# Hyena transform on one Trainium2 core: the first butterfly level and the last of the inverse summed in PSUM, and the output gate multiplied by x2 at the projection

## The chip, the core and the metric

The kernel runs on one core of one Trainium2 chip. The metric is the device time of one execution in microseconds (us); of several executions the median is taken. A core has TensorE (PE) for matmuls, VectorE (DVE), ScalarE (ACT) and GpSimd (POOL) for elementwise work, and DMA queues that SyncE (SP), ACT and POOL feed. Each engine works through its own list of instructions in order.

## What is computed

Two layers of a hybrid mixer over 1024 latent and 256 context tokens: an adaLN-modulated norm, one input projection whose columns feed four groups (a Hyena long convolution, an RWKV-7 scan, windowed and dense attention), a SiLU gate on each group's output, one output projection. The change concerns the Hyena group:

```python
def two_sided_fftconv(u, h_fwd, h_bwd, bias):
    ...
    U = jnp.fft.rfft(u, n=2 * L, axis=1)
    K = jnp.fft.rfft(k, n=2 * L, axis=0)
    y = jnp.fft.irfft(U * K[None], n=2 * L, axis=1)[:, :L]
    return y + u * bias

    zc = short_conv(z.astype(jnp.float32), conv_w.astype(jnp.float32))
    v, x1, x2 = jnp.split(zc, 3, axis=-1)
    y = x1 * two_sided_fftconv(v, h[:, 0, 0], h[:, 0, 1], bias[0])
    return x2 * two_sided_fftconv(y, h[:, 1, 0], h[:, 1, 1], bias[1])
```

The result of `hyena_branch` is multiplied by silu of its gate columns.

## The kernel before

**The stages of a layer.** `Proj` projects 128 columns at a time: three times eight matmuls per group of tokens (two groups of 512, and one of 256 in layer 0, which also carries the context), since each operand is split into a high and a low part (`chan`, L246). `conv` writes a block of short-convolved Hyena columns to `hy_d` in DRAM (blocks 0 and 1 are v, 2 and 3 are x1, 4 and 5 are x2); `gate` writes a block of gates to `gt_d`. Some of these blocks run beside the first RWKV stage (`phase_a`), four gate blocks beside the Hyena stage: `k.spread` ties each of their matmul groups to a mark that `k.mark` sets behind a Hyena matmul. After the Hyena stage come attention and the second RWKV stage.

**The Hyena stage** (`hyena`). A transform of length 2048 over 1024 tokens is cut into R = 8 residues of 128 tokens. The stage has four *units*: two convolutions (`o_`) times two halves of 128 channels (`hf`). One unit is

- `forward`: for each residue two 128x128 f32 matmuls with the tables `F` (L1394), cosine and sine, into PSUM banks of two residues. `pair` copies a bank to SBUF on ACT (L1211) and lets DVE form its sum and difference with the bank four residues on (L1213, L1215). `eight` does the other two butterfly levels on DVE (L1238 to L1242, then `odd`, L1227 to L1232, and `even`, L1219 to L1222) into `W`.
- the product with the filter's transform `Kf` on DVE (L1404 to L1407).
- back: four DVE sums and differences (L1410 to L1413), then `eight` again, *flipped*, into `Z`.
- `inverse`: for each residue two matmuls with the tables `IV` (L1436, or L1438 where the operands are swapped) and a DVE product with x1 (L1441) or, at the end, with the gate (L1443).

For the second convolution `inverse` loads the gate and x2 from DRAM and multiplies them on DVE (L1424); the result goes to `mix_d`.

The pool `sp` gives every tag a fixed number of buffers: the tag `s4`, of which `S`, `D` and `G` come, has two; `s2` (`AB`, `AB1`, `TU`) has five; a tile waits until the readers of the one before it in its buffer are done. PSUM has four banks here. The order on each engine is fixed when the program is built, by a scheduler. The rows below call a matmul of two f32 operands two records, so that eight matmuls of 128x128 read as x16.

In the text a *turn* is the stretch from one unit's flipped `eight` (its first instruction, L1238) to the next unit's; T is its start. There are three turns in a layer, six in all, and their places are those of the first view below.

Of the kernel before, what the change touches and what calls it, by code (L numbers as in the profile page):

```python
# [83 lines left out]
def setup(k, cp, dp):  # L84
# [23 lines left out]
    k.hy_d = dp.tile([768, TOK], F32, name="hy_d")  # L108
# [107 lines left out]
class Proj:  # L216
# [33 lines left out]
    def conv(w, blk, wi, dst, row, ctx, tanh_rows=0, pace=None):  # L250
# [19 lines left out]
    def gate(w, blk, row, ctx, pace):  # L270
# [898 lines left out]
def hy_consts(c):  # L1169
    f = np.float32  # L1170
    for nm, n, R in (("", L, R8), ("c", C, 2)):
# [14 lines left out]
        c["fw" + nm], c["iv" + nm] = np.ascontiguousarray(fw).astype(f), np.ascontiguousarray(iv).astype(f)  # L1186
        t = np.linspace(0.0, 1.0, n, dtype=f)[:, None]
# [10 lines left out]
class Dft:  # L1198
# [35 lines left out]
    def eight(s, out, S, D, flip):  # L1234
# [122 lines left out]
def hyena(k, l, kd, sp, pp):  # L1357
# [11 lines left out]
    for hf in range(2):  # L1369
        zc = tile_([2, n], "zc", 1)  # L1370
        nc.sync.dma_start(out=zc, in_=zd[:, 0:2, hf, 0:n])
        zv = zc.rearrange("q s (p r) -> q s r p", r=R)
# [9 lines left out]
    IV = tile_([R, 2, p], "IV", 1, p)  # L1382
    nc.sync.dma_start(out=IV, in_=A["iv"])

    def forward(o_, hf):
        u = U[hf]
        Kf = tile_([R, 2, 128], "Kf", 1, p)
        nc.sync.dma_start(out=Kf, in_=kd[o_, hf])

        def tr(rs):  # L1390
# [12 lines left out]
        t = tile_([R, 2, 128], "Z", 2, p)  # L1403
# [4 lines left out]
        Z = tile_([R, 2, 128], "Z", 2, p)  # L1408
# [5 lines left out]
        ft.eight(Z, S, D, True)  # L1414
        return Z

    def inverse(o_, hf, Z):
        if o_ == 0:
            u2 = tile_([R, 128], "u", 2, p)
        else:  # L1420
            gx = tile_([2, n], "zc", 1)
            nc.sync.dma_start(out=gx[:, 0], in_=k.gt_d[hf * 128:hf * 128 + 128, 0:n])
            nc.sync.dma_start(out=gx[:, 1], in_=zd[:, 2, hf, 0:n])
            TT(gx[:, 0], gx[:, 0], gx[:, 1], op=ALU.mult)  # L1424
            gv = gx[:, 0].rearrange("q (t r) -> q r t", r=R)
        for r0 in range(0, R, 4):
# [232 lines left out]
```

## Time and profile before

| | |
|---|---|
| median of 3 runs | 2482.23 us (2477.79 to 2485.27) |
| the profiled execution's own time | 2476.97 us |
| its span | 2475.0 us |
| PE busy | 2199.5 us (89%) |
| DVE busy | 1628.2 us (66%) |
| ACT busy | 1042.8 us (42%) |
| granted TensorE clock, mean | 0.938 of full speed |

The profile gives each instruction's start, its length and what ended the idle time ahead of it. Busy shares are means over stages that differ much, so a stage is read from its own rows: the windows view gives the busy time of each engine in a stretch, the timeline the instructions themselves. The column PEclk is the granted clock: 1.00 is 2.4 GHz, 0.50 is 1.2 GHz.

### The profile page before, as it was taken

The numbers are of one execution on the slowest core, as the hardware profiler recorded it, in microseconds if no ns is written. First come the engines' busy times: TensorE is split into PE (matmuls) and PEld (weight loads), VectorE is DVE, ScalarE is ACT, GpSimd is POOL, SyncE is SP. The second block draws the span as 40 slices with busy tenths as digits, with TensorE's granted clock in tenths as the row PEclk, the third lists the DMA queues.
The fourth block names the chain that finished last, engine by engine and source line by source line (L and its number), as shares of the span: only waits on it lengthen the run. The fifth ranks groups of instructions, "written<-read, shape, count | busy, mean of one in ns | idle before, by whom it ended". The sixth has DMA issues, their size and how long they took to land.

```text
span 2475.0 us, 44767 instructions
## 1 busy us (share of the span) xinstructions
PE 2199.5 (89%) x17048; PEld 1831.8 (74%) x17048; DVE 1628.2 (66%) x3913; ACT 1042.8 (42%) x2503; POOL 275.4 (11%) x408
## 2 busy tenths in 40 slices
PE   6799899999967799999898998989997659999898
PEld 3696689788756577886686887978776558877676
DVE  6975446578778566558543787565777886666753
ACT  5422233543210377666644322335432017766651
POOL 1000122100000000003122001321000000001212
PEclk9899999799988799999998998999898779999999
DMA  8225753676512646533443222445674155663432
GB/s 273 88 83 173 254 162 96 167 198 196 193 71 88 213 140 187 163 123 87 142 144 115 83 92 97 127 116 159 173 208 174 52 153 166 194 196 92 132 116 102
DMA packets 303763, 358.05 MB, mean 145 GB/s; under 512 B 121288, under 2 KB 245495, under 8 KB 298173
## 3 DMA queue, kind: packets, MB, share of 16 engines
q1 hardware_dynamic: 276712, 261.61, 34.7%
q0 software_dynamic: 11232, 70.78, 8.5%
q10 hardware_dynamic: 15604, 22.80, 2.9%
q8 instruction: 135, 2.21, 0.4%
q14 instruction: 80, 0.65, 0.1%
HBM read 226.27 MB, written 128.84 MB: 143 GB/s over the span
## 4 chain that ended last, share of the span: by engine, by line
PE 64%; DVE 11%; DMA 11%; ACT 5%; issue 4%; SPq 2%; POOL 0%; ACTq 0%; DVEq 0%; POOLq 0%
PE acc L246 16%; PE acc L340 9%; PE ops L1119 8%; PE O L1021 4%; PE pt L1011 3%; DMA st_d<-ST 3%; PE pk L1333 2%; PE S L980 2%; PE pr L1394 1%; PE S L981 1%; ACT P L995 1%; PE p_g L576 1%; PE mps L130 1%; DVE tmp L642 1%; DVE X L643 1%
## 5 line engine op out<-in xcount | busy, mean ns | idle before, releaser
L246 PE MATMUL acc<-hhi,wh 128*128 128x512 f32 (+1 forms) x896 | 218.5, 380 | 8.1 <-ACT wh L232 5.4
L246 PE MATMUL acc<-hlo,wh 128*128 128x512 f32 (+1 forms) x896 | 217.6, 375 | 0.0
L246 PE MATMUL acc<-hhi,wl 128*128 128x512 f32 (+1 forms) x896 | 208.8, 369 | 5.4 <-DVE wl L233 5.4
L985 DVE TENSOR_REDUCE st<-S 128x1 f32<-128x512 f32 (+1 forms) x320 | 171.8, 559 | 58.6 <-PE S L981 40.1
L995 ACT ACTIVATE P<-S,st 128x512 f32<-128x512 f32 (+1 forms) x320 | 184.1, 585 | 31.2 <-DVE st L988 26.5
L246 PEld LDWEIGHTS acc<-hhi,wh 128*128 128x128 f32 x896 | 158.5, 197 | 41.2 <-ACT wh L232 7.2
L246 PEld LDWEIGHTS acc<-hhi,wl 128*128 128x128 f32 x896 | 155.7, 190 | 33.4 <-DVE wl L233 5.7
L246 PEld LDWEIGHTS acc<-hlo,wh 128*128 128x128 f32 x896 | 157.9, 193 | 27.7 <-issue 1.7
L951 ACT COPY PT<-pt 128x512 f32<-128x512 f32 (+2 forms) x283 | 134.6, 501 | 84.2 <-PE pt L1011 83.1
L1011 PE MATMUL pt<-ident,P 128*128 128x128 f32 x976 | 158.4, 284 | 9.9 <-ACT P L995 6.5
L980 PE MATMUL S<-kp,qs 128*128 128x256 f32 (+2 forms) x384 | 141.4, 377 | 20.8 <-ACT P L995 19.4
L1011 PEld LDWEIGHTS pt<-ident,P 128*128 128x128 f32 x976 | 112.7, 143 | 39.4 <-issue 13.2
L1021 PE MATMUL O<-PT,V 128*64 128x256 f32 x976 | 135.3, 389 | 2.2 <-ACT PT L951 1.1
L981 PE MATMUL S<-kp,qs 128*128 128x256 f32 (+2 forms) x384 | 119.7, 325 | 2.9 <-DMA kp<-qk_d 2.9
L232 ACT ACTIVATE wh<-wr 128x1024 fp32r<-128x1024 f32 x58 | 60.9, 1058 | 104.9 <-PE acc L246 94.5
L980 PEld LDWEIGHTS S<-kp,qs 128*128 128x128 f32 x384 | 74.5, 194 | 40.4 <-ACT P L995 27.4
L1021 PEld LDWEIGHTS O<-PT,V 128*64 128x64 f32 x976 | 71.5, 138 | 43.6 <-issue 6.5
L258 ACT COPY zp<-acc 128x512 f32<-128x512 f32 (+1 forms) x66 | 34.6, 529 | 153.8 <-PE acc L246 107.8
L340 PE MATMUL acc<-wl,hhi 128*128 128x256 f32 x608 | 90.4, 289 | 5.5 <-POOL wl L233 5.5
L340 PE MATMUL acc<-wh,hhi 128*128 128x256 f32 x608 | 91.0, 291 | 2.0 <-ACT wh L232 2.0
L345 ACT ACTIVATE qx<-acc 128x256 f32<-128x256 f32 x76 | 29.2, 384 | 141.4 <-PE acc L340 139.9
L340 PE MATMUL acc<-wh,hlo 128*128 128x256 f32 x608 | 87.5, 285 | 0.0
(381 smaller groups left out, 5053.6 us busy)
## 6 DMA issues: line engine op xcount, KB each, us to landing
IN<-in_d POOLq DMA_DIRECT2D x18, 2048.0 KB, 9.7
wr<-in_w_in POOLq DMA_DIRECT2D x58, 512.0 KB, 4.6
mw<-in_mod_w SPq DMA_DIRECT2D x48, 512.0 KB
in_d<-BK SPq DMA_DIRECT2D x20, 512.0 KB
in_d<-AL SPq DMA_DIRECT2D x20, 512.0 KB
kp<-qk_d SPq DMA_DIRECT2D x32, 320.0 KB
qk_d<-qo SPq DMA_DIRECT2D x72, 128.0 KB
in_d<-GG SPq DMA_DIRECT2D x18, 512.0 KB
```

What stands on the lines that cost most here:

```text
L232: w.k.nc.scalar.activation(h, r, AF.Copy)
L246: nc.tensor.matmul(ps[:, :n], a[:, kc * 128:(kc + 1) * 128], b[:, kc, t0:t0 + n], start=(i == 0 and kc == 0), stop=(i == 2 and kc == 7))
L340: nc.tensor.matmul(ps[:, :256], x_[:, kc, t * 128:(t + 1) * 128], w_[:, kc, :], start=(n == 0 and kc == 0), stop=(n == 2 and kc == 7))
L951: nc.any.tensor_copy(o, i)
L980: nc.tensor.matmul(ps[:, w0:w0 + w], qs[:, hd % 2, hd // 2], kp[kv][0][:, t0:t0 + w], start=True, stop=False)
L981: nc.tensor.matmul(ps[:, w0:w0 + w], qs[:, hd % 2, hd // 2], kp[kv][1][:, t0:t0 + w], start=False, stop=not masks)
L985: TR(ng[:, i:i + 1], ps[:, :w0], axis=AX.X, op=ALU.max, negate=True)
L995: nc.scalar.activation(P[:, :w], ps[:, :w], AF.Exp, bias=gm, accum_out=den[:, i:i + 1])
L1011: nc.tensor.transpose(pt[:, i, :], P[:, i * 128:(i + 1) * 128], k.ident)
L1021: nc.tensor.matmul(O[kv * 64:kv * 64 + 64, 0], V[:, t, kv * 64:kv * 64 + 64], PTs[kv][:, i], start=(i == 0), stop=(i == nt - 1))
L1119: nc.tensor.matmul(ps, a[:, kc, :], b[:, kc, s], start=(n == 0 and kc == 0), stop=(n == 2 and kc == 7))
L1333: nc.tensor.matmul(ps[:, a, j], F[:, r, j, :], pm[j ^ dual][:, r, :], start=True, stop=True)
```

## The change

Forward: the sum and the difference of residues r and r + 4 are now formed in PSUM. For each of the first four residues two matmuls add u[r] and u[r + 4] (or its negative `un`, which ACT writes) into the same place, and ACT copies the bank to `S` or `D`; `pair` is no longer used here. Inverse: the flipped `eight` ends after its second level and returns `AB`, `AB1` and `G`; the last sums and differences are made by four matmuls a residue in place of two, with a second table of negated values `NIV`. `Z` is gone, so the matmuls read `s2` and `s4` tiles. The blocks of x2 stay in SBUF: `conv` returns the tile and `gate` multiplies the gate by it (new L280), in the order x2 block, its gate, x2 block, its gate; `hy_d` loses two of its six blocks, and the product in `inverse` goes. `zc` becomes two buffers of one row each.

```diff
     def gate(w, blk, row, ctx, pace, z=None):
...
+        if z is not None:
+            for t0, n, o in ((0, L, 1), (L, C, 3))[:2 if ctx else 1]:
+                nc.vector.tensor_tensor(gt[:, t0:t0 + n], gt[:, t0:t0 + n], z[:, t0 + o:t0 + o + n], op=ALU.mult)
...
     def eight(s, out, S, D, flip):
...
-        s.odd(out, TU, D[:, 0:2])
+        if not flip:
+            s.odd(out, TU, D[:, 0:2])
         s.TT(AB, S[:, 0::2], S[:, 1::2], op=ALU.add)
         s.TT(AB1, S[:, 0::2], S[:, 1::2], op=ALU.subtract)
-        s.even(out, AB, AB1[:, 0], AB1[:, 1])
+        if not flip:
+            s.even(out, AB, AB1[:, 0], AB1[:, 1])
+            return
+        G = s.twiddled(TU, D[:, 0:2])
+        return (AB[:, 0], AB[:, 1]), (AB1[:, 0], AB1[:, 1]), (G[:, 0, 0], G[:, 0, 1]), (G[:, 1, 0], G[:, 1, 1])
...
+        un = tile_([R // 2, 128], "un", 1, p)
+        nc.scalar.activation(un, u[:, R // 2:], AF.Copy, scale=-1.0)
+
+        def tr(out, rs, far):
+
             ps = bank("pr").rearrange("p (r j e) -> p r j e", r=2, j=2)[:p]
             for a, r in enumerate(rs):
                 for j in range(2):
-                    nc.tensor.matmul(ps[:, a, j], F[:, r, j, :], u[:, r, :], start=True, stop=True)
+                    nc.tensor.matmul(ps[:, a, j], F[:, r, j, :], u[:, r, :], start=True, stop=False)
+                    nc.tensor.matmul(ps[:, a, j], F[:, r + R // 2, j, :], far[:, r, :], start=False, stop=True)
             k.mark(1.0)
-            return ps
+            nc.scalar.activation(out, ps, AF.Copy)
...
-        ft.pair(S[:, 2:4], D[:, 2:4], tr((1, 3)), tr((5, 7)))
-        ft.pair(S[:, 0:2], D[:, 0:2], tr((0, 2)), tr((4, 6)))
+        tr(D[:, 2:4], (1, 3), un)
+        tr(D[:, 0:2], (0, 2), un)
+        tr(S[:, 0:2], (0, 2), u[:, R // 2:])
+        tr(S[:, 2:4], (1, 3), u[:, R // 2:])
...
-            gx = tile_([2, n], "zc", 1)
-            nc.sync.dma_start(out=gx[:, 0], in_=k.gt_d[hf * 128:hf * 128 + 128, 0:n])
-            nc.sync.dma_start(out=gx[:, 1], in_=zd[:, 2, hf, 0:n])
-            TT(gx[:, 0], gx[:, 0], gx[:, 1], op=ALU.mult)
-            gv = gx[:, 0].rearrange("q (t r) -> q r t", r=R)
+            gx = tile_([n], "zc", 2)
+            nc.sync.dma_start(out=gx, in_=k.gt_d[hf * 128:hf * 128 + 128, 0:n])
+            gv = gx.rearrange("q (t r) -> q r t", r=R)
...
-                for j in range(2):
-                    iv, x = IV[:, r0 + a, j, :], Z[:, BACK[r0 + a], j, :]
...
+                jobs = [(IV[:, r, j, :], P[:, j]) for j in range(2)] + [(neg(i, j), Q[:, m]) for i, j, m in x]
+                for i, (iv, x) in enumerate(jobs):
                     if o_ == 0:
-                        nc.tensor.matmul(ps[:, a], iv, x, start=(j == 0), stop=(j == 1))
+                        nc.tensor.matmul(ps[:, a], iv, x, start=(i == 0), stop=(i == 3))
...
-                    first = [("h", i) for i in range(6)] + [(0, i) for i in range(2)]
+                    first = [("h", i) for i in range(4)] + [("h", 4), (0, 0), ("h", 5), (0, 1)]
```

**The order on PE, the first turn of layer 0**, before. `pi` are banks of the inverse, `pr` banks of the next unit's forward transform, `acc` projection groups of the gate blocks:

```order
L246 MATMUL acc<-hlo,wh 128x512 x8
L246 MATMUL acc<-hhi,wl 128x512 x8
L1436 MATMUL pi<-Z,IV 128x128 x4
L1394 MATMUL pr<-u,F 128x128 x8
L1436 MATMUL pi<-Z,IV 128x128 x12
L1394 MATMUL pr<-u,F 128x128 x8
L246 MATMUL acc<-hhi,wh 128x256 x8
```

After the change the same place begins so (`s_6620` and `s_6621` are `AB` and `AB1`):

```order
L246 MATMUL acc<-hhi,wl 128x512 x8
L1466 MATMUL pi<-s_6620,IV 128x128 x6
L1466 MATMUL pi<-s_6620,NIV 128x128 x2
L1417 MATMUL pr<-u,F 128x128
L1418 MATMUL pr<-un,F 128x128
L1417 MATMUL pr<-u,F 128x128
L1418 MATMUL pr<-un,F 128x128
L1466 MATMUL pi<-G,IV 128x128 x2
L1466 MATMUL pi<-G,NIV 128x128
L1466 MATMUL pi<-G,IV 128x128
L1466 MATMUL pi<-s_6621,IV 128x128 x2
L1466 MATMUL pi<-s_6621,NIV 128x128
```

and, behind the rest of the inverse (32 matmuls in all) and of the forward transform (32, of which four stand in the middle above), ends so:

```order
L1418 MATMUL pr<-u,F 128x128
L1417 MATMUL pr<-u,F 128x128
L1418 MATMUL pr<-u,F 128x128
L246 MATMUL acc<-hhi,wh 128x256 x8
L246 MATMUL acc<-hlo,wh 128x256 x8
L246 MATMUL acc<-hhi,wl 128x256 x8
```

Before, half of the next unit's 16 forward matmuls stood ahead of most of the inverse, and 32 in all stood between the projection groups. Now all but four of its 32 forward matmuls stand behind the last of the inverse, and 64 stand between the projection groups.

**The order on DVE, the same turn**, before, from the last two instructions of `odd`'s first step to the next unit's first level (`s_66..` are `S`, `D` and `s2` tiles):

```order
L1227 SCALAR_TENSOR_TENSOR G<-s_6603,s_6596 128x512
L1228 SCALAR_TENSOR_TENSOR G<-s_6603,s_6596 128x512
L1221 TENSOR_TENSOR Z<-s_6602 128x2x128
L1222 TENSOR_TENSOR Z<-s_6602 128x256
L1231 TENSOR_TENSOR Z<-G 128x2x2x128
L1232 TENSOR_TENSOR Z<-G 128x2x256
L1213 TENSOR_TENSOR s_6641<-s_6653,pr 128x512
L1215 TENSOR_TENSOR s_6642<-s_6653,pr 128x512
L1441 TENSOR_TENSOR u<-pi,x 128x512 x2
L1238 TENSOR_TENSOR s_6673<-s_6642 128x256
L1239 TENSOR_TENSOR s_6673<-s_6642 128x256
L1213 TENSOR_TENSOR s_6641<-s_6667,pr 128x512
```

and now, from the flipped `AB` on:

```order
L1256 TENSOR_TENSOR s_6620<-s_6614 128x512
L1257 TENSOR_TENSOR s_6621<-s_6614 128x512
L1236 SCALAR_TENSOR_TENSOR G<-s_6622,s_6615 128x512
L1237 SCALAR_TENSOR_TENSOR G<-s_6622,s_6615 128x512
L1471 TENSOR_TENSOR u<-pi,x 128x512 x2
L1252 TENSOR_TENSOR s_6716<-s_6673 128x256
L1253 TENSOR_TENSOR s_6716<-s_6673 128x256
L1256 TENSOR_TENSOR s_6714<-s_6672 128x512
L1257 TENSOR_TENSOR s_6715<-s_6672 128x512
L1229 TENSOR_TENSOR W<-s_6714 128x256
L1230 TENSOR_TENSOR W<-s_6714 128x256
L1236 SCALAR_TENSOR_TENSOR G<-s_6716,s_6673 128x512
```

The ten instructions that wrote `Z` and formed the first level are gone. Between `G` and the next unit's second level DVE now has only the two products with x1 (L1471), and `AB` (L1256) of the next unit stands directly ahead of everything but `TU` (L1252, L1253).

## Rows read from the trace of the kernel before

**Rows 1.** Windows view, the six turns: each engine's busy us (instructions), PEclk, DMA share, GB/s.
```profile
714.02:744.04 30.02, 23.05 (x136) 20.84 (x136) 27.20 (x44) 3.81 (x6) 0.00 (x0) 0.89 0.15 56
744.04:773.52 29.48, 26.23 (x160) 24.16 (x160) 26.15 (x43) 3.14 (x6) 0.00 (x0) 0.88 0.16 57
773.52:805.11 31.59, 20.94 (x112) 18.71 (x112) 28.35 (x48) 2.37 (x4) 0.00 (x0) 0.85 0.37 104
1930.48:1961.07 30.59, 21.16 (x112) 18.96 (x112) 26.78 (x43) 3.43 (x5) 0.00 (x0) 0.78 0.15 52
1961.07:1990.82 29.75, 26.68 (x136) 23.51 (x136) 25.75 (x42) 2.96 (x5) 0.00 (x0) 0.86 0.15 43
1990.82:2024.21 33.39, 14.37 (x88) 13.05 (x88) 28.40 (x51) 1.77 (x3) 0.00 (x0) 0.75 0.56 162
```

**Rows 2.** Timeline, DVE and one ACT row, second turn of layer 0: start, us, engine, line, [idle before].
```profile
744.04 0.42 DVE L1238 TENSOR_TENSOR s<-s 128x256 f32<-128x256 f32 x1
...
745.31 0.68 DVE L1242 TENSOR_TENSOR s<-s 128x512 f32<-128x512 f32 x1
...
747.18 0.69 DVE L1228 SCALAR_TENSOR_TENSOR G<-s,s 128x512 f32<-128x512 f32 x1
...
751.70 0.69 DVE L1213 TENSOR_TENSOR s<-s,pr 128x512 f32<-128x512 f32 x1 [1.96 <-PE pr L1394]
...
754.31 0.69 DVE L1441 TENSOR_TENSOR u<-pi,x 128x512 f32<-128x512 f32 x1 [0.65 <-PE pi L1436]
...
755.20 0.59 ACT L1211 COPY s<-pr 128x512 f32<-128x512 f32 x1 [4.29 <-PE pr L1394]
...
756.77 0.68 DVE L1215 TENSOR_TENSOR s<-s,pr 128x512 f32<-128x512 f32 x1
...
773.52 0.42 DVE L1238 TENSOR_TENSOR s<-s 128x256 f32<-128x256 f32 x1
```

**Rows 3.** Timeline, PE, the same turn.
```profile
746.48 2.05 PE L1436 MATMUL pi<-Z,IV 128*128 128x128 f32 x8 [7.01 <-DVE Z L1219]
...
748.32 3.27 PE L1394 MATMUL pr<-u,F 128*128 128x128 f32 x16
...
751.43 2.84 PE L1436 MATMUL pi<-Z,IV 128*128 128x128 f32 x24
...
754.11 1.95 PE L1394 MATMUL pr<-u,F 128*128 128x128 f32 x16
...
755.81 1.20 PE L246 MATMUL acc<-hhi,wh 128*128 128x256 f32 x8
```

**Rows 4.** Timeline, first unit of layer 0 (two rows) and of layer 1 (two rows).
```profile
686.48 1.06 PE L1394 MATMUL pr<-u,F 128*128 128x128 f32 x8
...
693.07 1.23 DVE L1424 TENSOR_TENSOR zc<-zc 128x1024 f32<-128x1024 f32 x1 [16.05 <-DMA zc<-hy_d]
...
1906.47 4.57 PE L1394 MATMUL pr<-u,F 128*128 128x128 f32 x32
...
1911.87 1.23 DVE L1424 TENSOR_TENSOR zc<-zc 128x1024 f32<-128x1024 f32 x1 [0.44 <-DMA zc<-hy_d]
```

**Rows 5.** Windows view, 4 us stretches of the same turn.
```profile
744.00:748.00 4.00, 1.52 (x7) 1.55 (x8) 4.00 (x10) 0.00 (x0) 0.00 (x0) 0.53 0.04 15
...
752.00:756.00 4.00, 4.00 (x38) 4.00 (x37) 3.02 (x6) 0.59 (x1) 0.00 (x0) 1.00 0.02 4
```

**Rows 6.** Timeline of layer 0's last unit and what follows; last row from the chain.
```profile
797.26 6.16 SPq L932 DMA_DIRECT2D kp<-qk_d  x8
...
811.11 5.23 PE L1438 MATMUL pi<-IV,Z 128*128 128x128 f32 x24 [1.27 <-DVE Z L1232]
...
816.38 1.07 DVE L1443 TENSOR_TENSOR zc<-pi,zc 128x512 f32<-128x512 f32 x1 [1.20 <-PE pi L1438]
...
817.49 0.36 PE L980 MATMUL S<-kp,qs 128*128 128x256 f32 x1 [1.15 <-DMA qs<-qk_d]
...
821.06 19.32 DMA zc<-hy_d
```

More of the change, by code (lines that the diff above doesn't have):

```diff
@@ L268, in conv, with gate @@
             nc.sync.dma_start(out=dst[row:row + 128, 1024:TOK], in_=o[:, 1027:1283])
-    def gate(w, blk, row, ctx, pace):
+    def gate(w, blk, row, ctx, pace, z=None):
         k, nc, sp = w.k, w.k.nc, w.sp
@@ L284, in beside @@
     def beside(w, todo, part=None):
+        z = None
         ctx = not w.last
@@ L1186, in hy_consts @@
         c["fw" + nm], c["iv" + nm] = np.ascontiguousarray(fw).astype(f), np.ascontiguousarray(iv).astype(f)
+        if not nm:
+            at = [BACK.index(x) for x in range(R)]
+            c["niv"] = np.stack([-c["iv"][:, at[x], 1 - x % 2] for x in range(2, R)] + [-c["iv"][:, at[1], j] for j in range(2)], 1)
         t = np.linspace(0.0, 1.0, n, dtype=f)[:, None]
@@ L1222, in even, with twiddled @@
         s.TT(o[:, 5:7], A1[:, ::-1], B1, op=ALU.subtract)
-    def odd(s, out, TU, CD):
-        o = out.rearrange("p s j e -> p (s j) e")
+    def twiddled(s, TU, CD):
         G = s.sp.tile([128, 2, 2, 2, 128], F32, tag="s4", bufs=2, name="G")
@@ L1228, in odd @@
         s.STT(G[:, 1], TU, -RT, CD, op0=ALU.mult, op1=ALU.add)
+        return G
+    def odd(s, out, TU, CD):
+        o = out.rearrange("p s j e -> p (s j) e")
+        G = s.twiddled(TU, CD)
         g, h = G[:, :, 0], G[:, :, 1]
@@ L1369, in hyena @@
     for hf in range(2):
[L1370 to L1372 removed]
         for s, lst in ((0, U), (1, X1)):
+            zc = tile_([n], "zc", 2)
+            nc.sync.dma_start(out=zc, in_=zd[:, s, hf, 0:n])
+            zv = zc.rearrange("q (p r) -> q r p", r=R)
             u = tile_([R, 128], "ux"[s], 2, p)
@@ L1381, in hyena @@
         yield
-    IV = tile_([R, 2, p], "IV", 1, p)
+    IV, NIV = tile_([R, 2, p], "IV", 1, p), tile_([R, p], "NIV", 1, p)
     nc.sync.dma_start(out=IV, in_=A["iv"])
+    nc.sync.dma_start(out=NIV, in_=A["niv"])
     def forward(o_, hf):
@@ L1413, in forward @@
         TT(S[:, 2:4], W[:, 4:6], W[:, 6:8], op=ALU.add)
-        ft.eight(Z, S, D, True)
-        return Z
+        return ft.eight(None, S, D, True)
     def inverse(o_, hf, Z):
@@ L1432, in inverse @@
             for a in range(4):
-                for j in range(2):
-                    iv, x = IV[:, r0 + a, j, :], Z[:, BACK[r0 + a], j, :]
+                r, place = r0 + a, BACK[r0 + a]
+                g, h = place // 2, place % 2
+                neg = lambda i, j: NIV[:, place - 2 if g else 6 + j] if i else IV[:, r, j, :]
+                if g == 0:
+                    (P, Q), x = (Z[0][0], Z[0][1]), [(h, 0, 0), (h, 1, 1)]
+                else:
+                    P, Q = Z[g]
+                    x = [(h, 0, 1), (1 - h, 1, 0)]
+                jobs = [(IV[:, r, j, :], P[:, j]) for j in range(2)] + [(neg(i, j), Q[:, m]) for i, j, m in x]
+                for i, (iv, x) in enumerate(jobs):
                     if o_ == 0:
-                        nc.tensor.matmul(ps[:, a], iv, x, start=(j == 0), stop=(j == 1))
+                        nc.tensor.matmul(ps[:, a], iv, x, start=(i == 0), stop=(i == 3))
                     else:
-                        nc.tensor.matmul(ps[:, a], x, iv, start=(j == 0), stop=(j == 1))
+                        nc.tensor.matmul(ps[:, a], x, iv, start=(i == 0), stop=(i == 3))
             k.mark(2.0)
@@ L1446, in inverse @@
         else:
-            nc.sync.dma_start(out=k.mix_d[hf * 128:hf * 128 + 128, 0:n], in_=gx[:, 0])
+            nc.sync.dma_start(out=k.mix_d[hf * 128:hf * 128 + 128, 0:n], in_=gx)
     for o_ in range(2):
@@ L1512, in ctx_hyena @@
     zd = k.hy_d.rearrange("(s h p) t -> p s h t", h=2, p=128)
-    zc = tile_("zc", [3, 2, C])
-    for s in range(3):
+    zc = tile_("zc", [2, 2, C])
+    for s in range(2):
         nc.sync.dma_start(out=zc[:, s], in_=zd[:, s, :, L:TOK])
     gx = load(tile_("gx", [2, C]), k.gt_d[0:256, L:TOK].rearrange("(h p) t -> p h t", p=128))
-    TT(gx, gx, zc[:, 2], op=ALU.mult)
     ux = []
```

14 lines of the change are left out of this document (7 added, 7 removed).

## The prediction, made before the changed kernel was run

> **What bounds the kernel now.** I read the windows view of the Hyena stages first, then DVE's timeline of one turn, then PE's timeline beside it. On the average PE looks like the bound (89% of the span), but the Hyena stages are another matter: in the six turns DVE is busy for 25.8 to 28.4 of 29.5 to 33.4 us, PE for 14.4 to 26.7 [rows 1]. So a turn is DVE's, and that is what the change goes at. But PE is not far behind: 26.2 of 29.5 us in the second turn, at a granted clock of 0.88.
>
> The timeline shows where DVE does stop [rows 2]. T is 744.04. DVE works without a gap through the flipped `eight`, stops 1.96 us at 751.70 for the next unit's forward matmuls and 0.65 us at 754.31 for the inverse, and has finished the next unit's first level at 756.77 + 0.60 = 757.37, that is T + 13.3. From there to the next T, 773.52, it has work for 16.15 us, three or four gate products among it. PE starts the inverse at 746.48 and is through with inverse and forward at 756.06 [rows 3]: 32 matmuls in some 9.6 us, nearly all of it covered by DVE's own work on `Z`, the first level and the products with x1. **That cover is what the change removes together with the work.**
>
> What a matmul costs depends on the clock. The 24 records at 751.43 take 2.84 us, 0.237 us for each of 12 matmuls; the 24 ahead of them, 746.48 to 751.43, need 4.95 us, because PE had stood idle 7 us and comes back at the lower level: PEclk is 0.53 in the first 4 us and 1.00 from 752 [rows 3, 5]. At the lower level all along, 12 matmuls take 5.23 us, 0.436 us each [rows 6].
>
> **The change, part by part.**
>
> *What DVE loses.* A unit loses the four instructions of `pair`, the two of `odd`'s second step and the four of `even` in the flipped `eight`: 6 of 512 columns, which follow each other every 0.60 us, and 4 of 256, every 0.34: 5.0 us a unit, 40 us over eight units. That is the gain if nothing takes their place.
>
> *What PE gains.* 16 forward and 16 inverse matmuls more in a unit, 256 in all: at 0.237 us 61 us of PE. They are not free even beside DVE: the second turn's 26.2 us of PE would come to about 32 with 7.6 us more and the lower clock taken out, against a turn of 29.5.
>
> *A turn after the change.* The order says what must follow what. DVE makes `TU` and `AB`: in the trace the third instruction after T starts at 745.31, so `AB` stands at T + 1.27 [rows 2]. PE starts at about T + 1.4 with eight inverse matmuls that need only `AB`, then four forward ones, 24 inverse ones (`G` stands at T + 3.2, in time) and 28 forward ones: 64 with nothing between. At 0.237 us they end at T + 16.6. ACT copies the last bank: 0.59 us as in 755.20 [rows 2], with some 0.3 us for the two hand-overs (an estimate from the gaps of 0.1 to 0.2 us between these rows). `AB` of the next unit reads all of `S`, and the rest of DVE's list stands behind it, so DVE goes on at T + 17.5. `TU` and the products with x1 are done by then. The instructions from there to the next T are those of before, 16.15 us. So the first level stands at T + 17.5 in place of T + 13.3: **+4.2 us a turn, +25.2 us for six**, if PE has its full clock. Of DVE's 5.0 us nothing is left, since it waits.
>
> *The clock.* PE will come back from idle at the lower level in four of the six turns: in the third turn of each layer 96 or 72 projection matmuls follow the forward transform and last until 2 us before the next inverse; in the others it stands idle for 5 us or more by the same reckoning, and I take it to come back as it did after the 7.01 us at 746.48. The lower level cost 4.95 - 2.84 = 2.1 us there [rows 3]; it then was partly hidden, now it all lies on the path: 4 x 2.1 = +8.4. Its ends are 0 and 6 x 2.1 = 12.6.
>
> *The product with x2.* L1424 takes 1.23 us of DVE in the third turn of each layer: -2.4. In the first units it costs more: in layer 0 DVE stood at 693.07 for the load of x2, although the first sum's bank was ready before; in layer 1 it waited 0.44 us [rows 4].
>
> *The first units.* Layer 0: forward starts at 686.48 [rows 4] and T was 714.02 [rows 1], 27.5 us. Now 32 matmuls of 0.237, 0.9 for the copy and 16.15: 24.7, and 0.3 for a short lower clock: -2.5. Layer 1: 1906.47 to 1930.48 was 24.0 us; now the same, 24.6, and 0.9 for four matmuls at the lower level: +1.5. Together -1.
>
> *The tail.* The last unit's inverse runs alone. In layer 0 it ended 11.2 us after T (811.11 + 5.23 against 805.11) at the lower level [rows 1, 6]. Now 32 matmuls from T + 1.4: 15.4 us at the lower level all along, 12.2 if the second half runs at 0.237. I take +2 a layer, +4; the ends are 0 and 8.
>
> *At the projection.* L280 adds 1.23 us of DVE twice a layer (and 0.4 for the context in layer 0), beside projection matmuls that keep PE busy. I cost it at nothing; without that cover it is at most 6. Where `z` is held, the two `zo` buffers alternate as before.
>
> *Queues.* On SP the loads of v and x1 are four of 0.5 MB and `NIV` is one more of 0.5 MB a layer, ahead of `Kf` and the second half's loads; the two gate loads stand ahead of the later `Kf` loads and wait for transposes only. All that is issued while PE still works on projections: nothing, at most 2 us. Behind the stage, the context's Hyena part loads two blocks, not three, out of a wait of 19.32 us [rows 6]: -1, at most -3.
>
> Is a longer stage paid in full? In layer 0 the attention's first matmul waits for loads of `qs` that follow the loads of `kp`, and those were issued at 797.26, when the last projection group was done [rows 6]. That group is tied to the Hyena matmuls by its marks and so moves with them: yes.
>
> **The sum:** 25.2 + 8.4 - 2.4 - 1 + 4 - 1 = +33 us. The profiled execution took 2476.97 us, so 2510; it lies 5.3 us under the median of the runs, 2482.2, so I forecast **2515 us** for the median.
>
> **The rivals.**
>
> *The clock stays up.* Twice the matmuls might keep PE busy enough that it no longer falls to the lower level between units. Then the 8.4 us and half of the tail go: +23, 2505 us. For it: the full clock from 752 on, once PE is busy [rows 5]. Against it: the projections are no more than before and the turn gets longer, so there still are idle stretches like the 7.01 us at 746.48 [rows 3]. The Trainium skill has this rule in "TensorE: Matmul & The Clock Gate", section "What's actually happening": the throttled state is the default and activity releases it. The rows agree that it rises with work and falls with idleness; the rule would speak for this rival, with its +23.
>
> *The delay is swallowed behind layer 0.* There the chain waits 19.32 us for loads [rows 6]. If these came no later than now, layer 0's share, half of the sum, would vanish: +17, 2499 us. Against it: the loads are issued behind the last projection.
>
> *Gain and loss cancel.* A turn breaks even where 64 matmuls take 11 us, 0.172 us each. Neither row has such a price, but if the scheduler's order let DVE work ahead by a few us it would come to the same: within 7 us of 2482.
>
> *Faster: a matmul that adds into PSUM costs half.* If the second of two that go to the same place cost about one record, 0.118 us, the second half of the 64 would be 3.8 us shorter; if all did, 7.6 us: DVE's wait would end at T + 9.9, -3.4 a turn, -20 in six, with the other terms -25: 2457 us. It decides below 0.172 us. Against it: the inverse of before already adds two matmuls into each place, and its 0.237 us is the price of just that [rows 3].
>
> **How the numbers follow.** The forecast, PE's chain with the clock falling in most turns: 0.52. Clock up: 0.20. Swallowed: 0.13. Cancelled: 0.08. Faster: 0.07. About 0.3%, 7 us, is what a measurement of this kernel can tell from no change. So faster 0.07, same 0.08, slower 0.85. The range reaches down to the swallowed case and half of the way to no change, 2491, and up to 2532, where the lower clock and the tail take their upper bounds (+4, +4) and DVE waits 1.5 us more a turn for projection groups that now end later.
>
> **What would show it.** The turns grow to about 36 us, with DVE busy about 22 of them and one wait of some 12 us at the next unit's `AB` (L1256) or `TU` (L1252), put down to ACT L1420 or PE L1418. L1213 and L1215 with `pr` and L1424 are gone; PE has 512 more records of 128x128. The forecast is wrong if the DVE wait ahead of the second level is under 8 us, if the 64 matmuls of a turn take less than 13 us, or if the stage grows and the span doesn't.

## The result, and the profile after

The kernel became slower: 2527.9 us median (2516.9 to 2536.6), beside 2483.8 us (2477.8 to 2485.8) for the kernel before, both in four runs. The ratio is **1.0152, with a 95% interval of 1.0114 to 1.0190**, which is +38 us (28 to 47); the two medians themselves lie 44 us apart. The profiled execution of after has a span of 2515.1 us against 2475.0 us, 40.1 us more; it was the fastest of its four runs.

The first line of the page shows what was exchanged, work of DVE for work of PE:

```profile
PE 2253.6 (90%) x17560; PEld 1884.6 (75%) x17560; DVE 1591.4 (63%) x3837; ACT 1057.1 (42%) x2524; POOL 276.6 (11%) x408
```

PE has 17,560 matmul records where it had 17,048, which is the 512 of 256 more matmuls, and 54 us more of busy time. DVE has 37 us less. PE's share rose from 89% to 90%, and the time rose too.

The windows view of the six turns, after (span, then busy us and instructions of PE, PEld, DVE, ACT, POOL, then PEclk, DMA share, GB/s). It answers to [rows 1]:

```profile
721.33:758.49 37.16, 31.13 (x200) 28.92 (x200) 22.38 (x34) 5.55 (x9) 0.00 (x0) 0.87 0.12 47
758.49:793.33 34.84, 32.53 (x224) 30.46 (x224) 21.32 (x32) 4.87 (x9) 0.00 (x0) 0.94 0.13 49
793.33:826.38 33.05, 25.47 (x176) 23.23 (x176) 22.37 (x37) 3.59 (x6) 1.84 (x2) 0.97 0.20 54
1960.63:1996.73 36.10, 28.13 (x176) 25.91 (x176) 21.95 (x33) 5.17 (x8) 0.00 (x0) 0.88 0.13 45
1996.73:2030.64 33.91, 32.41 (x200) 29.46 (x200) 20.81 (x31) 4.10 (x7) 0.00 (x0) 0.92 0.13 45
2030.64:2063.49 32.85, 20.21 (x153) 18.72 (x152) 22.24 (x39) 3.58 (x6) 1.84 (x2) 0.89 0.35 96
sum 207.91, PE 169.88 PEld 156.70 DVE 131.08 ACT 26.86 POOL 3.69; mean PE 28.31 PEld 26.12 DVE 21.85 ACT 4.48 POOL 0.61
```

DVE is busy for 21 to 22 us of a turn, where it was busy for 26 to 28, and the turn is longer, not shorter: 207.9 us for six, against 184.8 in [rows 1], so +23.1. DVE was the engine that filled a turn; now neither is full.

Where DVE stands still, in its timeline of the first of these turns (start, duration, engine, line, tile; in brackets the idle time ahead of it and what ended it). It answers to [rows 2], one turn earlier:

```profile
721.33 0.42 DVE L1252 TENSOR_TENSOR s<-s 128x256 f32<-128x256 f32 x1
...
723.93 0.69 DVE L1237 SCALAR_TENSOR_TENSOR G<-s,s 128x512 f32<-128x512 f32 x1
731.24 0.69 DVE L1471 TENSOR_TENSOR u<-pi,x 128x512 f32<-128x512 f32 x1 [6.62 <-PE pi L1466]
733.92 0.69 DVE L1471 TENSOR_TENSOR u<-pi,x 128x512 f32<-128x512 f32 x1 [1.99 <-PE pi L1466]
735.49 0.43 DVE L1252 TENSOR_TENSOR s<-s 128x256 f32<-128x256 f32 x1 [0.88 <-ACT s L1420]
...
740.80 0.69 DVE L1256 TENSOR_TENSOR s<-s 128x512 f32<-128x512 f32 x1 [4.55 <-ACT s L1420]
741.41 0.69 DVE L1257 TENSOR_TENSOR s<-s 128x512 f32<-128x512 f32 x1
```

Four waits, 6.62 + 1.99 + 0.88 + 4.55 = 14.0 us, stand between T and the next unit's `AB`; those that [rows 2] shows come to 2.6 us. The first two, 8.6 us, stand ahead of the products with x1, which wait for the inverse; the last ends at `AB`. And what PE did meanwhile:

```profile
722.79 2.90 PE L1466 MATMUL pi<-s,IV 128*128 128x128 f32 x12 [7.97 <-issue]
725.49 1.06 PE L1466 MATMUL pi<-s,NIV 128*128 128x128 f32 x4
...
739.30 0.39 PE L1418 MATMUL pr<-u,F 128*128 128x128 f32 x2
739.52 0.39 PE L1417 MATMUL pr<-u,F 128*128 128x128 f32 x2
739.75 0.39 PE L1418 MATMUL pr<-u,F 128*128 128x128 f32 x2
739.89 1.20 PE L246 MATMUL acc<-hhi,wh 128*128 128x256 f32 x8
```

One chain of 64 matmuls runs without a stop from 722.79 to 739.89, and DVE's next `AB` (L1256, 740.80) comes 0.9 us behind its end. The duration of a record overlaps the next; the starts are 0.22 us apart, for the first product into a place (L1417) and for the one added to it (L1418) alike.

Over all eight units, the groups of DVE instructions (name, shapes, count, busy us, mean ns) with the idle time ahead of them in us, and what ended it:

```profile
L1256 DVE TENSOR_TENSOR s<-s 128x512 f32<-128x512 f32 x16 | 11.1, 691 | 36.5 <-ACT s L1420 36.5
L1252 DVE TENSOR_TENSOR s<-s 128x256 f32<-128x256 f32 x16 | 6.8, 424 | 30.8 <-ACT s L1420 30.8
L1471 DVE TENSOR_TENSOR u<-pi,x 128x512 f32<-128x512 f32 x8 | 5.5, 692 | 31.8 <-PE pi L1466 31.8
```

The three kinds of wait come to 99 us. Before, in the kernel's own lines, two kinds stood in their place:

```profile
L1213 DVE TENSOR_TENSOR s<-s,pr 128x512 f32<-128x512 f32 x16 | 11.0, 686 | 21.5 <-PE pr L1394 21.3
L1441 DVE TENSOR_TENSOR u<-pi,x 128x512 f32<-128x512 f32 x8 | 5.5, 692 | 3.0 <-PE pi L1436 3.0
```

That is 24.5 us, and 17 us more stood ahead of the product with x2, nearly all in the first unit of layer 0 [rows 4]. The change took 37 us of work off DVE and gave it some 58 us of waiting.

Of the 40.1 us between the two spans, 23.1 lie in the six turns. The rest, from the starts of the same lines in both traces: 3.7 up to the last `p_w` matmul of layer 0, 3.6 from there to the first T, 1.8 from the last T to the attention, 7.0 from the last `p_w` of layer 1 to the last copy of the solve, 4.6 from there to T, 0.5 behind the last T, 0.3 to the end; attention and all between the layers came out 4.6 shorter. No edit touches the code of the 3.7. In the 7.0 and the -4.6 there are edits, of the gate part: the products of L280 in layer 1 start at 1847.02 and 1883.42, and the context's Hyena part has one load and one product less. But the 7.0 is a stretch of 106.3 us before and 113.3 after, and over the profiled executions of this study, before and after among them, it takes 100.2 to 113.3 us, both ends of that in kernels with the gate part (e6 and the changed one). I take these three for variation, which is not shown for each of them; the other terms come to some 34 us.

### The profile page after: what moved, and what is told of

Its sections match the earlier page's. It is cut to its first block, busy times and chain, and to the rows that moved or that the text cites. A ratio compares the mean times of both kernels' runs of the same rounds, so it can differ in the third digit from the quotient of the medians.

```text
span 2515.1 us, 45718 instructions
## 1 busy us (share of the span) xinstructions
PE 2253.6 (90%) x17560; PEld 1884.6 (75%) x17560; DVE 1591.4 (63%) x3837; ACT 1057.1 (42%) x2524; POOL 276.6 (11%) x408
## 4 chain that ended last, share of the span: by engine, by line
PE 68%; DMA 11%; DVE 9%; ACT 5%; issue 4%; SPq 1%; POOL 0%; ACTq 0%; DVEq 0%; POOLq 0%
PE acc L246 18%; PE acc L347 9%; PE ops L1126 8%; PE O L1028 4%; PE pt L1018 3%; DMA st_d<-ST 2%; PE p_g L583 2%; PE S L987 2%; PE pk L1352 2%; ACT P L1002 2%; PE pi L1466 1%; PE S L988 1%; DMA zc<-hy_d 1%; PE pr L1417 1%; PE pr L1418 1%
## 5 line engine op out<-in xcount | busy, mean ns | idle before, releaser
L1002 ACT ACTIVATE P<-S,st 128x512 f32<-128x512 f32 (+1 forms) x320 | 184.2, 585 | 29.5 <-DVE st L995 24.8
L1018 PEld LDWEIGHTS pt<-ident,P 128*128 128x128 f32 x976 | 113.3, 143 | 37.9 <-issue 13.2
L352 ACT ACTIVATE qx<-acc 128x256 f32<-128x256 f32 x76 | 29.2, 385 | 144.6 <-PE acc L347 144.6
```

The costliest lines, as they stand in the source:

```text
L1002: nc.scalar.activation(P[:, :w], ps[:, :w], AF.Exp, bias=gm, accum_out=den[:, i:i + 1])
L1018: nc.tensor.transpose(pt[:, i, :], P[:, i * 128:(i + 1) * 128], k.ident)
```

## The experiments

The theory (**A**): the matmuls are added at a place where DVE has nothing to do but wait for them, so the loss is their chain's length. The main rival (**B**): the change has other DMA issues in another order, SP's loads come late, and the loss is ahead of the stage. Further rivals: it is the added PE work as such, or the clock.

**e1: the gate part alone** (before, with the edits of that part; these are the main ones):

```diff
-    k.hy_d = dp.tile([768, TOK], F32, name="hy_d")
+    k.hy_d = dp.tile([512, TOK], F32, name="hy_d")
...
+                nc.vector.tensor_tensor(gt[:, t0:t0 + n], gt[:, t0:t0 + n], z[:, t0 + o:t0 + o + n], op=ALU.mult)
...
-            nc.sync.dma_start(out=gx[:, 1], in_=zd[:, 2, hf, 0:n])
-            TT(gx[:, 0], gx[:, 0], gx[:, 1], op=ALU.mult)
```

> The kernel before with the gate part alone: hy_d of 512 rows, the product of gate and x2 at the projection, the order of the projections and one load less in inverse; the transform stays on DVE. Theory A (the transform's PE chain makes the loss): the turns keep their 30 us, the third turn of each layer loses the 1.2 us of the product: 2478 to 2484 us. Theory B (the other number and order of DMA issues makes the loss, through SP's waits ahead of the stage): the stage begins some 9 to 12 us later over the two layers: 2493 us or more.

Measured: 2485.4 us, ratio 0.9993 (0.9970 to 1.0016).

**e2: the transform alone**, the same edits undone in the changed kernel, and v and x1 of a half again in one load.

> The changed kernel with the gate part undone: hy_d of 768 rows, x2 loaded and multiplied in inverse, v and x1 in one load, the projections' old order; both transform levels in PSUM. Theory A: six turns of +4 us and the x2 product back on DVE, where it now falls into DVE's wait: 2507 to 2520 us. Theory B: 2484 to 2492 us.

Measured: 2520.2 us, ratio 1.0131 (1.0094 to 1.0169); its six turns take 213.6 us. The two together: the gate part is worth nothing that can be measured, and the whole loss is the transform's. The fewer stores and the missing loads of x2, a part of B's reason, are in e1 as well and do nothing there; the separate loads of v and x1 are not, and e4 goes at those.

**e3: half of the forward sum left out**, in the changed kernel:

```diff
-                    nc.tensor.matmul(ps[:, a, j], F[:, r, j, :], u[:, r, :], start=True, stop=False)
-                    nc.tensor.matmul(ps[:, a, j], F[:, r + R // 2, j, :], far[:, r, :], start=False, stop=True)
+                    nc.tensor.matmul(ps[:, a, j], F[:, r, j, :], u[:, r, :], start=True, stop=True)
```

> The changed kernel without the second matmul of each forward place (it leaves out half of the forward sum): 16 matmuls less in a unit, all else as it was. Theory A (DVE waits for PE's chain): at 0.223 us a matmul 3.6 us less in each of six turns and two first units, 28 us: about 2499 us, turns of 30 to 33 us. If DVE's own work or the queues set the turn: no change, 2520 to 2530 us.

Measured: 2495.4 us, ratio 1.0039 (1.0017 to 1.0060), that is 28 us under the changed kernel's 1.0152. Its turns in layer 0, in the windows view:

```profile
718.04:750.27 32.23, 26.21 (x168) 24.00 (x168) 22.37 (x33) 5.56 (x9) 0.00 (x0) 0.92 0.14 52
750.27:782.54 32.27, 29.95 (x192) 27.89 (x192) 21.33 (x33) 4.87 (x9) 0.00 (x0) 0.90 0.14 52
782.54:813.44 30.90, 23.33 (x144) 21.11 (x144) 22.37 (x36) 3.58 (x6) 1.91 (x2) 0.91 0.21 59
```

DVE's work is the same to 0.01 us as in the changed kernel, and PE has 16 matmuls less in a turn (32 records), so this version leaves out a part of the transform. The turns of layer 0 are 9.7 us shorter in sum, where 16 matmuls less at 0.223 us would make 10.7. So it is PE's chain that DVE's time hangs on, not its own work.

**e4: one load for v and x1**, in the changed kernel:

```diff
-            zc = tile_([n], "zc", 2)
-            nc.sync.dma_start(out=zc, in_=zd[:, s, hf, 0:n])
+        zc = tile_([2, n], "zc", 1)
+        nc.sync.dma_start(out=zc, in_=zd[:, 0:2, hf, 0:n])
```

> The changed kernel with v and x1 of a half loaded by one DMA into one tile, as before, which takes two issues off SP and gives the later loads another place in the rotation. Theory B: the second half's transposes no longer wait 10 and 22 us for their load, 3 to 7 us less: about 2521 us. Theory A: the turns stay at 36, 34 and 33 us, and what is gained is at most those 7 us: 2520 to 2528 us.

Measured: 2528.0 us, ratio 1.0165 (1.0142 to 1.0187): no gain that the runs show, though the load itself did come earlier. In the changed kernel, in layer 1, the last copy of the solve, the second half's load and its transposes lie like this (timelines of DVE, SP's queue and PE, in order of time):

```profile
1926.80 0.68 DVE L652 COPY XR<-X 32x1024 f32<-32x1024 f32 x1
1928.80 1.03 SPq L1391 DMA_DIRECT2D zc<-hy_d  x2
1932.33 1.94 PE L1397 MATMUL pd<-ident,zc 128*128 128x128 f32 x8 [22.29 <-DMA zc<-hy_d]
```

and in e4:

```profile
1917.37 0.38 SPq L1390 DMA_DIRECT2D zc<-hy_d  x1
1928.78 0.68 DVE L652 COPY XR<-X 32x1024 f32<-32x1024 f32 x1
1930.49 3.68 PE L1397 MATMUL pd<-ident,zc 128*128 128x128 f32 x16 [18.64 <-ACT u L1398]
```

From the solve's copy to the first unit's first `eight` it is 12.4 us after, 8.3 in e4 and 9.4 before. Why the load came late in the changed kernel is in the waits of SP's queue in this stretch: it is put down to a store of the solve, which the load does not read.

```profile
SPq L1391 <- DMA ys_d<-X: 15.7, 1, 15.7
```

From the last `p_w` matmul of layer 0 to the first T it is 151.1 us before, 154.7 after and 151.1 in e4, and from the solve's copy to T in layer 1 it is 29.2, 33.8 and 29.7. So with e4 both stages begin as early as before, and the loss is still there: B falls as its cause. The late loads cost up to some 8 us in these traces; whether the whole kernel pays them is open, since the intervals of e4 and of the changed kernel leave room for a gain of 8 us.

**e5: a third `s4` buffer.** The first `eight` of a unit makes `TU`, then `AB`, then `G`, though `G` needs no `S`: with two `s4` buffers it takes the one that holds `S`, and so stands behind `AB`. In the changed kernel:

```diff
-        return s.sp.tile([128, int(tag[1]), 2, 128], F32, tag=tag, bufs={"s2": 5, "s4": 2}[tag], name=tag)[:, :n]
+        return s.sp.tile([128, int(tag[1]), 2, 128], F32, tag=tag, bufs={"s2": 5, "s4": s.n4}[tag], name=tag)[:, :n]
...
-    ft = Dft(k, sp)
+    ft = Dft(k, sp, 3)
...
-        un = tile_([R // 2, 128], "un", 1, p)
+        un = ft.tl(2).rearrange("p s j e -> p (s j) e")
```

> The changed kernel with a third s4 buffer in the Hyena stage (un takes an s2 buffer to make room), so that G of a unit's first eight no longer has to wait for AB to release S, and the order puts odd's four instructions ahead of AB. Theory A (DVE waits for PE's chain at AB): 4 x 0.60 = 2.4 us of DVE's work move from behind the wait into it, in six turns and two first units: 19 us less, about 2508 us, with AB as late after T as before. If the turn were set by DVE's sum or by PE's sum, moving work within DVE's list would change nothing: 2520 to 2530 us.

Measured: 2514.2 us, ratio 1.0108 (1.0064 to 1.0152). Its turns take 96.0 and 97.5 us in the two layers, 14.5 less in sum; expected for them were 6 x 2.4 = 14.4. Turn by turn it is 6.1, 1.9, 1.1, 2.5, 0.9 and 1.9 us, so the agreement of the sums is in part luck. What carries the argument is the wait at `AB` over the eight units, 36.5 us in the changed kernel and now

```profile
L1256 DVE TENSOR_TENSOR s<-s 128x512 f32<-128x512 f32 x16 | 11.0, 690 | 7.6 <-ACT s L1420 7.6
```

with 7.8 us in its place ahead of `G`. The same instructions in another place are worth 2.4 us a turn on the mean, because the place is a wait. The intervals of e5 and of the changed kernel overlap, so the traces carry this one.

**e6 and e10: one half each**, on the kernel with the gate part: the forward level in PSUM alone, or the inverse level alone (48 matmuls a turn in place of 32 or 64). e6 is the kernel of e1 with this edit of `forward` (`tr` as in the change); e10 is the changed kernel with the same edit undone:

```diff
-        ft.pair(S[:, 2:4], D[:, 2:4], tr((1, 3)), tr((5, 7)))
-        ft.pair(S[:, 0:2], D[:, 0:2], tr((0, 2)), tr((4, 6)))
+        tr(D[:, 2:4], (1, 3), un)
+        tr(D[:, 0:2], (0, 2), un)
+        tr(S[:, 0:2], (0, 2), u[:, R // 2:])
+        tr(S[:, 2:4], (1, 3), u[:, R // 2:])
```

> The kernel before with the gate part and the forward half of the transform change; the inverse keeps its last level on DVE (16 matmuls, Z in SBUF). Theory A: PE has 48 matmuls in a turn, 10.7 us at 0.223, from about T + 2.4, when the first part of Z stands: AB at about T + 14.3 against the first level at T + 13.3 before, so +1 us a turn: 2488 to 2498 us, a small part of the loss. If the loss were the forward half's alone, or in proportion to the matmuls added: half of it or more, 2503 us or more.

> The changed kernel with the forward level back on DVE: the gate part and the inverse half alone (48 matmuls a turn), in the old order. Theory A: PE starts at T + 1.4 and needs 10.7 us for 48, T + 12.1; the copy, the last two sums and the hand-overs follow, T + 14.5 against T + 13.3 before: +1 to +2 us a turn, 2488 to 2500 us. With e6 at +8 us the two halves then make less than the whole's +38, since each half alone still lies mostly beside DVE's work. If each matmul cost the same wherever it lies: half of +38, 2505 us.

Measured: e6 2495.9 us, 1.0033 (1.0010 to 1.0056); e10 2493.7 us, 1.0026 (1.0004 to 1.0047). Some 8 and 6 us; together 15, where both at once cost 38 (28 to 47). That would fit matmuls of which the first 16 lie beside DVE's work and the next 16 do not. The traces do not show it. The sums over the six turns, of e6 and then of e10:

```profile
sum 197.19, PE 153.55 PEld 140.44 DVE 145.82 ACT 27.09 POOL 0.00; mean PE 25.59 PEld 23.41 DVE 24.30 ACT 4.52 POOL 0.00
sum 194.16, PE 151.83 PEld 138.67 DVE 145.31 ACT 17.50 POOL 3.83; mean PE 25.30 PEld 23.11 DVE 24.22 ACT 2.92 POOL 0.64
```

DVE is idle for 51.4 and 48.9 us of them, where it was 22.2 before and 76.8 with both halves: each half alone brings about half of the wait. The turns are 12.4 and 9.3 us longer than before, together 21.7, with both halves 23.1. So in the turns the halves nearly add up; where the rest of the 38 lies is open. The +1 us a turn that was expected of e6 is +2.1.

**e7, e8, e9: the same arithmetic in another order.** If the chain's place is the trouble, it can be moved. The forward matmuls of a unit need nothing of the unit before it, only of the one before that. So they are written one unit earlier (`head`), into two buffers `h4` of their own, and the products of a unit's inverse stand behind the next unit's first `eight`:

```diff
-    for o_ in range(2):
-        for hf in range(2):
-            Z = forward(o_, hf)
-            inverse(o_, hf, Z)
-            yield
+    heads, inv = [head(0), head(1)], None
+    for i, (o_, hf) in enumerate(units):
+        b = body(o_, hf, *heads[i])
+        next(b)
+        if inv:
+            next(inv, None)
+            if i + 1 < 4:
+                heads.append(head(units[i + 1][1]))
+        Z = next(b)
+        inv = inverse(o_, hf, Z)
+        next(inv)
+        yield
+    next(inv, None)
```

To make room, `G` of the first `eight` and `S` and `D` of the flipped one lie in the tile of the product with `Kf` while that is free. e7 has both levels in PSUM (64 matmuls), e8 the forward one alone (48), e9 none (32).

> The changed kernel with the same arithmetic in another order: the forward matmuls of a unit are written one unit earlier, its S and D lie in two buffers of their own, and the products of a unit's inverse stand in DVE's list behind the next unit's first eight. Theory A: the chain of 64 matmuls is then beside DVE's work again; a turn is PE's 15.2 us and 11 to 17 us of projections, or DVE's 22 us and some waits, 27 to 30 us in place of 33 to 37: some 35 us less, 2480 to 2500 us. If the loss came from the added PE work itself or from the clock, the order would not matter: 2515 to 2530 us.

> The same order with the forward half and the gate part alone (48 matmuls a turn, the last inverse level on DVE). Theory A: DVE has 24 to 25 us a turn and PE 10.7 and 11 to 17 us, so turns of 26 to 28 us where before had 30: 2460 to 2480 us, under before. If DVE's saved work is worth nothing even when it does not wait: 2480 us or more.

> The early order of e7 and e8 and the gate part, with both levels of the transform on DVE as before (32 matmuls a turn): what the order is worth by itself. Theory A: a turn is DVE's own work, 26 to 28 us of the rows of before less the product with x2, where e7 has 22 and e8 25: some 4 us a turn under before, 2458 to 2470 us, so that most of e7's gain is the order and the rest the sums in PSUM. If PE's sum were what limits all three, this one with the least PE work would be the fastest: under 2450 us. If the order alone were nothing: 2480 us or more.

Measured: **e7 2451.3 us, 0.9868 (0.9829 to 0.9908); e8 2457.9 us, 0.9887 (0.9847 to 0.9927); e9 2458.6 us, 0.9901 (0.9864 to 0.9938).** All three beat both kernels, e7 by more than was expected. The six turns of e7:

```profile
713.51:735.28 21.77, 21.77 (x152) 20.10 (x151) 21.73 (x34) 3.04 (x5) 0.00 (x0) 1.00 0.20 79
735.28:756.50 21.22, 21.22 (x167) 20.22 (x167) 19.93 (x30) 5.08 (x8) 0.00 (x0) 1.00 0.14 50
756.50:779.64 23.14, 23.14 (x163) 21.41 (x162) 22.79 (x34) 3.46 (x7) 0.95 (x1) 1.00 0.13 52
1917.62:1940.15 22.53, 22.53 (x161) 20.85 (x160) 21.68 (x33) 4.49 (x7) 0.00 (x0) 1.00 0.20 71
1940.15:1962.26 22.11, 22.11 (x154) 20.28 (x154) 21.50 (x33) 2.80 (x6) 0.00 (x0) 1.00 0.20 72
1962.26:1984.40 22.14, 22.14 (x147) 20.08 (x146) 21.42 (x31) 3.17 (x6) 0.95 (x1) 1.00 0.12 48
```

PE is busy for all of every turn, DVE for all but 0.04 to 1.3 us, and the turn is 21 to 23 us in place of 33 to 37. I had expected 27 to 30, since I took the projections that lie in a turn to be bound to it; the order lets them run later. DVE's timeline of the first of these turns shows how the wait went:

```profile
715.38 0.69 DVE L1257 TENSOR_TENSOR s<-t 128x512 f32<-128x512 f32 x1
715.98 0.42 DVE L1252 TENSOR_TENSOR s<-h 128x256 f32<-128x256 f32 x1
...
724.54 0.69 DVE L1480 TENSOR_TENSOR u<-pi,x 128x512 f32<-128x512 f32 x1
725.14 2.29 DVE L1435 TENSOR_TENSOR t<-W,Kf 128x2048 f32<-128x2048 f32 x1
727.34 0.69 DVE L1480 TENSOR_TENSOR u<-pi,x 128x512 f32<-128x512 f32 x1
```

Here `t` is the tile of the product with `Kf`, `h` one of the `h4` buffers. The next unit's `TU` (L1252 from `h`) starts 0.6 us behind the present unit's `AB1`, since its `S` and `D` lie ready, and the inverse's products (L1480) find their banks full.

The turns of e9 in layer 0:

```profile
723.14:749.51 26.37, 20.78 (x124) 19.04 (x125) 26.34 (x42) 3.22 (x5) 0.00 (x0) 0.87 0.18 67
749.51:774.49 24.98, 20.67 (x126) 18.42 (x124) 24.95 (x42) 2.76 (x5) 0.00 (x0) 0.93 0.13 43
774.49:799.93 25.44, 14.81 (x80) 12.51 (x80) 25.25 (x48) 1.20 (x2) 0.00 (x0) 0.90 0.38 121
```

Here DVE is full, at 25 us, 4 more than in e7: this is what the sums in PSUM save once DVE does not wait for them. But over the whole kernel it is not seen: e9 stands at 0.9901 and e7, run again in the same set (e11), at 0.9885, well inside each other's intervals. Behind the stage e7 gives it back. The timelines of PE and of SP's queue, the last projection matmuls of the stage and the loads of `kp` that follow them:

```profile
801.16 1.98 PE L246 MATMUL acc<-hhi,wl 128*128 128x512 f32 x8
803.17 14.49 SPq L939 DMA_DIRECT2D kp<-qk_d  x8
```

In e9 they start at 788.60 and 790.73 (in the kernel before at 795.25 and 797.26, in the changed one at 818.66 and 820.67). So e7's last T, 779.64, is 20 us ahead of that of e9, but PE, which has 32 matmuls more in each of four units (28.5 us at 0.223), is through with the projections 13 us later, and the attention, whose loads these are, starts at 831.9 against 813.3. As far as this shows, DVE's saved time is worth nothing in a stretch where PE is the engine that is late.

**e11 and e12**: e7 again, and e7 with the one load of e4.

> e7 again, beside e12 and with more rounds: ratio to before within 0.983 to 0.991.

> e7 with v and x1 of a half in one load, as in e4: whether SP's late loads of the second half cost anything. If the transposes' wait of 22 us in layer 1 lies on the path for the 7 us by which the first unit comes later: 2444 us, 7 us less than e11. If what comes behind takes it up: the same as e11 within 4 us.

Measured: e11 2459.0 us, 0.9885 (0.9853 to 0.9917); **e12 2448.0 us, 0.9847 (0.9810 to 0.9884)**, the fastest version of all. Over six runs of each their means differ by 10.5 us, with an interval of 3 to 18 worked out from the scatter of the runs (5.0 and 6.5 us). The expectations were 7 us or next to nothing. Why there is a gain is open: in the profiled execution of e12 the second half's load in layer 1 is still issued only behind the solve's copy (2.45 us, in e11 2.50), and the stretch that is shorter, 100.2 us from the last `p_w` to that copy against 110.6, is the one that varies by as much between kernels whose code there is the same.

## Why the prediction was right

2515 us was forecast, with 2491 to 2532 as its range, and 2527.9 came out; +33 us was the sum, where the ratio makes it +38 (28 to 47). The direction, the mechanism and the place were as argued. The size is in part luck: the stretches for which the sum had turns, first units and tail grew by 23.1 - 1.2 + 2.3 = 24 us, for 34 forecast. The other 16 of the 40 lie where the sum had next to nothing: 9.5 ahead of the first forward matmuls of the two layers, and 6.4 in the stretches of 3.7, 7.0, -4.6 and 0.3 us. By its steps:

*A turn after the change.* Right in its path: what holds DVE last is the next unit's `AB`, released by ACT's copy of the last bank. The wait itself looks otherwise than forecast. It was to be one of some 12 us at `AB` or `TU`, with the products with x1 done by then, and the forecast called itself wrong if the wait ahead of the second level were under 8 us; but in the first turn only 4.55 us stand at `AB` and 0.88 at `TU`, and 8.6 of the 14.0 ahead of the products with x1. Read by those two rows alone that sign would have fired; the time from T to `AB`, which the sum uses, is not touched by it. `AB` was to stand at T + 17.5 at full clock; it stands at T + 19.5, 18.1, 17.0 in layer 0 and 19.3, 18.4, 17.5 in layer 1. That the 5.0 us saved on DVE would all be waited away was right as well (e3, e5). Taken as a whole the six turns were forecast at 6 x (17.5 + 16.15) + 8.4 - 2.4 = 207.9 us, and 207.9 were measured. That the two agree so closely is luck: `AB` came 3.6 us earlier in the sum of the six than forecast, and the stretches from `AB` to the next T took 98.1 us in place of 94.5. What was off is the base: the step took +4.2 us from the second turn, whose first level stood at T + 13.3, for all six. The other five were longer before, 184.8 us in sum and not 6 x 29.5 = 176.9 [rows 1]. So of the forecast 31.2 us only 23.1 came.

*The clock.* Right. The chain of 64 took 17.1, 15.6 and 14.3 us in layer 0, 17.0, 16.0 and 14.3 in layer 1. At 0.223 us a matmul it is 14.3, so the lower level of 1.2 GHz cost 2.8, 1.4 and 0 and then 2.7, 1.7 and 0: 8.6 us over the six, for 8.4 forecast, and in four of the six turns, as forecast. The matmul itself at the full 2.4 GHz is 0.223 us, not 0.237, which gave 5.4 us back. The forecast had read 0.237 us from the length of a record, 2.84 us for 12; from the start of these to the start of the next (751.43 to 754.11, [rows 3]) it is 0.223 there too. The granted clock of the turns is 0.87 to 0.97: ahead of the four chains that began at the lower level PE had stood idle for 6.1 to 12.7 us (7.97 ahead of the first), ahead of the other two for 2.6 and 2.1.

*The product with x2, L280.* The gate part as a whole is nothing that can be measured, as e1 shows; forecast were -2.4 and 0.

*First units and tail.* From the first `pr` matmul to T: 27.5 to 26.0 us in layer 0 and 24.0 to 24.4 in layer 1, -1.2 for -1 forecast. From the last T to the attention +2.3, for +4, but not for the reason given: the inverse of the last unit did not get longer in layer 0, where it ended 10.4 us after T against 11.2, since its second half now ran at the full clock. What grew there is a wait behind it, 3.81 us of PE ahead of the attention where it was 1.15.

*Queues.* Mis-sized: "nothing, at most 2 us". SP's loads of the second half stood behind its own waits (15.7 us for the solve's store), and the stretches ahead of the first forward matmul grew by 5.2 us in layer 0 and 4.3 in layer 1; e4, by its times to the first T, takes this back. How much of it the whole kernel pays is open (e4, e12).

*The rivals.* That the clock stays up did not happen here, but it does in e7, where PE has no idle time and PEclk is 1.00 in all six turns, with the same 64 matmuls. The Trainium skill, in "TensorE: Matmul & The Clock Gate", section "What's actually happening", says that activity releases the throttle; the trace agrees, and shows that activity is a matter of order: twice the work in a lump with an idle time ahead did not do it. That the delay is swallowed behind layer 0 fell: the attention's first matmul went from 817.49 [rows 6] to 840.6. That an added matmul costs half fell: L1417 and L1418 each take 0.22 us. That gain and loss cancel fell: it needed 64 matmuls in 11 us, and they took 14.3 to 17.1. The loss came from where the matmuls lie, not from their number: with 256 more of them than before, e7 is 33 us faster than before.

The Trainium skill says in "Perfetto Trace Analysis", section "Optimization Strategies", that the goal in general is to keep the Matmul engine as highly utilized as possible. Here PE's share rose by a point, from 89% to 90%, and the kernel got slower by 1.5%: the share was raised by work that was not there before, in a place where another engine waited for it.

## What to carry to other kernels

Before work is moved from a full engine to one with time left, ask what the full engine has to do while the other one works: the order of the instructions decides this, not the shares. If the first thing behind the moved work needs its result, the work is no longer hidden, and what was saved is spent on waiting. Look first for work that is ready earlier than the order lets it run (here the forward transform of a unit, which needs only the unit before the last): issuing it earlier gave 1.0% with the transform's arithmetic as it was and the gate part, which alone gave nothing, and with that done the sums in PSUM added nothing that these runs can show. Compare a forecast of a repeated stretch with the sum of all its repeats, not with the one that was read. And when a total comes out as forecast, compare its terms too: here the largest was a quarter too high, and stretches that it had left out made up for it.

## What was not expected

- The order alone was worth 25 us (e9), in a kernel whose DVE looked full in this stage. Its three turns of layer 0 take 76.8 us against 91.1 [rows 1]: 9.1 of the 14.3 are idle time of DVE, 9.4 before and 0.25 now, and 5.2 are work of DVE that now lies elsewhere, the product with x2 (1.2) and steps of projections.
- Two buffers that take turns put an instruction behind a wait that it does not need: `G` behind `AB`, 2.4 us a turn on the mean (e5).
- PE at full clock and without a stop takes 64 float32 matmuls of 128x128 in 14.3 us, 0.223 us from start to start, whether each adds to a place or begins one.
- In e7 a stage that ended 47 us earlier than in the changed kernel (last T of layer 0, 779.6 against 826.4) brought the attention's first matmul only 9 us forward (831.9 against 840.6): the projections that had been spread over the turns came behind them.
